# Moving 32 sums of weight quarters from VectorE to GpSimd at the turn between two groups, with a new order of copies and weighings on ScalarE

## The chip, the cores and the metric

The kernel runs on one core of one Trainium2 chip. The metric is the device time of one execution in microseconds (us), as the median over the runs; a profile of one execution stands beside it. The span of a profile is some 1.8 us shorter than the time.

## The reference

```python
def reference(x, w):                       # x: 8 x 2048 x 2048, w: 2048 x 2048, float32
    cs = np.cumsum(x, axis=1)
    diff = cs - shifted(cs)                # cut: the cumulative sum, less itself one row earlier
    return np.matmul(diff, w)
```

The difference of a cumulative sum is x again, so the kernel computes x times w: 16384 rows by 2048 by 2048.

## The kernel before

The kernel multiplies in 2x2 blocks with seven products in place of eight. A group is four row tiles of 128 rows, taken as two block rows. From the second group on, three of the seven products are themselves cut in 2x2, again with seven products; these need sums of the quarters of three weight blocks, B21, B22 and T4. Each set has 16 sums of 128 x 512 float16, made once, at the turn from the first group (`group_plain`) to the second (`second` in `group`).

Names: A11 to A22, B11 to B22 and C11 to C22 are blocks of x, w and the result. S1 to S4 are sums of blocks of x ("row sums"), T1 to T4 sums of blocks of w, Q1 to Q4 sums of the quarters of a weight block. X, Y, Z and V are pairs of PSUM banks, into which the products go (tile `b` in the profile; weights are `W`, quarter sums also `inner`). g and h mark the first row tile of each block row, u and v are row scales.

The engines: TensorE multiplies. ScalarE copies a product out of PSUM with a row scale ("keep"), weighs a row tile (sum of absolute values, which gives the row scales) and narrows it to float16. VectorE adds further products into the kept tile ("add") and makes all sums. The parts that matter, with cuts marked:

```python
    def keep(dst, ps, scale):                       # ScalarE, L497
        for c, p in pieces_of(dst, ps):
            after("act", lambda: nc.scalar.activation(c, p, COPY, scale=scale))
    def add(dst, ps, scale):                        # VectorE, L502: PSUM in, one SBUF tensor in
        ...
    def total(dst, p, q, op):                       # VectorE, L511: row sums S1, S2, ...
        after("dve", lambda: nc.vector.tensor_tensor(dst.all, p.all, q.all, op))
    def less(dst, p, q):                            # VectorE, L515: sums of weights, two SBUF tensors in
        for k in range(len(dst)):
            after("dve", lambda: nc.vector.tensor_tensor(dst[k], p[k], q[k], SUB))
    def less_in(Q1, Q2, Q4, t11, t12, t21, t22):    # 12 sums of a block's quarters
        less(Q1, t12, t11); less(Q2, t22, Q1); less(Q4, t21, Q2)
    def less_in3(Q1, Q2, Q4, t11, t12, t21, t22):   # 4 more, in place: Q3
        less(t12, t22, t12)
    def new_c(slot):                                # a tile of C in one of four slots
        return cpool.tile([P, NH], f32, name=f"c{slot}")
    ...
    # first group, near its end
    add(C22, X, vg)
    put(C22, g + 1, 1)                              # store of C22, slot d
    ...
    less(T4, B21, T2)
    product(Z, S1, T1, True)
    ...
    weigh(g + 5, c)                                 # waits for the load of row tile g + 5
    scale_of(g + 5)
    C22 = new_c(d)                                  # slot d again
    keep(C22, Z, vh)
    ...
    less_in(*in2); less_in3(*in2)                   # B21
    product(Z, S4h, B22, False)
    ...
    less_in(*in3)                                   # B22
    ...
    # second group
    product(X, A11g, B11, True)
    units[g], units[h] = unit(g), unit(h)           # scales u, on VectorE
    keep(C11g, X, ug)
    S3g = sums(g, S4g)                              # four row sums, S2 among them
    weigh(h + 1, c); ready(h + 1); less_in(*in4)    # T4
    ...
    product(X, S2, T2, False)
```

`after` keeps each engine's instructions in the order of the program, so an engine that waits for one instruction holds up all that stand behind it.

Of the kernel before, what the change touches and what calls it, by code (L numbers as in the profile page):

```python
# [33 lines left out]
def kernel(  # L34
# [6 lines left out]
    nc = tc.nc  # L41
# [12 lines left out]
    ADD = mybir.AluOpType.add  # L54
    SUB = mybir.AluOpType.subtract
    MUL = mybir.AluOpType.mult
    MAX = mybir.AluOpType.max
    AX = mybir.AxisListType
# [21 lines left out]
    B11, T1, B12, T2, B21, T3, B22, T4 = (  # L80
        [p[:, i // 2, i % 2] for p in pieces] for i in range(8)
    )
# [51 lines left out]
    def after(engine, ask):  # L134
        if engine in last:
            with tc.issue_after(last[engine].ins):
                said = ask()
        else:
            said = ask()
        last[engine] = said[-1] if isinstance(said, tuple) else said  # L140
        return said


    with tc.tile_pool(name="ring", bufs=7) as ring, tc.tile_pool(
# [97 lines left out]
        def put(c, rows, columns, queue=nc.gpsimd):  # L242
            return queue.dma_start(out2[rows, columns], c)
# [31 lines left out]
        for ko in range(KO - KQ):  # L275
# [9 lines left out]
            if ko in turns:  # L285
                q, a = turns[ko]
# [32 lines left out]
        x4, _ = after("sp", lambda: bring(PLAIN))  # L319
        x6, _ = after("sp", lambda: bring(PLAIN + 2))  # L320
# [25 lines left out]
        got = {}  # L346
# [68 lines left out]
        m = small.tile([P, 1], f32, name="m")  # L415
# [9 lines left out]
        x7, _ = after("sp", lambda: bring(PLAIN + 3))  # L425
# [39 lines left out]
    def product(ps, a, b, first):  # L465
        for k in range(KH):
            for n in range(NH // NB):
                nc.tensor.matmul(  # L468
                    ps[n],
                    a[k],  # L470
                    b[k][:, n, :],
                    start=(first and k == 0),
                    stop=(k == KH - 1),
                    skip_group_check=True,
                )
# [19 lines left out]
    def keep(dst, ps, scale):  # L495
        for c, p in pieces_of(dst, ps):
            after("act", lambda: nc.scalar.activation(c, p, COPY, scale=scale))  # L497
# [12 lines left out]
    def total(dst, p, q, op):  # L510
        after("dve", lambda: nc.vector.tensor_tensor(dst.all, p.all, q.all, op))  # L511

    def less(dst, p, q):
        for k in range(len(dst)):
            after("dve", lambda: nc.vector.tensor_tensor(dst[k], p[k], q[k], SUB))  # L515


    def less_in(Q1, Q2, Q4, t11, t12, t21, t22):
        less(Q1, t12, t11)
        less(Q2, t22, Q1)  # L520
        less(Q4, t21, Q2)

    def less_in3(Q1, Q2, Q4, t11, t12, t21, t22):
        less(t12, t22, t12)

    def new_c(slot):
        return cpool.tile([P, NH], f32, name=f"c{slot}")
# [5 lines left out]
    def fetch_x(t):  # L533
        if t < END:
            came[t], _ = after("sp", lambda: bring(t))

    def weigh(t, slot):
        if t < END:
            xf = came.pop(t)
            m, _ = after("act", lambda: measure(xf, new_c(slot)))  # L540
            got[t] = m, None, xf


    def weigh_in(t, ps):
        if t < END:
            xf = came.pop(t)
            m = small.tile([P, 1], f32, name="m")
            m4 = small.tile([P, 4], f32, name="m4")
            for i in range(4):
                at = ds(i * NB, NB)  # L550
                after(
                    "act",
                    lambda: nc.scalar.activation(  # L553
                        ps[i % 2],
                        xf[:, at],
                        ABS,
                        scale=1.0 / ROW,
                        accum_out=m4[:, i : i + 1],
                    ),
                )  # L560
            after("dve", lambda: nc.vector.tensor_reduce(m, m4, AX.X, ADD))  # L561
            got[t] = m, None, xf

    def scale_of(t):
        if t < END:
            m, _, xf = got[t]
            s, _ = after("dve", lambda: invert(m))
            came[t] = xf, s

# [25 lines left out]
    def sums_in(a, b, first, second):  # L595
        a11, a12, a21, a22 = a.half(0), a.half(1), b.half(0), b.half(1)
        s1, s2, s3, s4 = (p.half(n) for p in (first, second) for n in range(2))

        def half_one():
            total(s1, a21, a22, ADD)  # L600
            total(s2, s1, a11, SUB)

        def half_two():
            total(s3, a11, a21, SUB)
            total(s4, a12, s2, SUB)

        return half_one, half_two, (a11, a12, a22, s1, s2, s3, s4)
# [39 lines left out]
    def group_plain(g, X, Y, Z, V, a, b, c, d):  # L647
        h = g + 2
        ug, uh = unit(g), unit(h)
        A11g, A12g = parts(g)  # L650
        A11h, A12h = parts(h)
        A21g, A22g = parts(g + 1)
        product(X, A11g, B11, True)
        for k in range(3):
            block(B22, 1, 1, k, "act")
        C11g = new_c(a)
        keep(C11g, X, ug)
        for k in range(3, KH):
            block(B22, 1, 1, k, "act" if k < 6 else "dve")
        product(V, A12g, B21, True)  # L660
        product(Y, A11h, B11, True)
        add(C11g, V, ug)
        put(C11g, g, 0)

        less(T3[:2], B22[:2], B12[:2])
        total(S1, A21g, A22g, ADD)
        product(Z, A12h, B21, True)
        weigh(h + 1, d)
        C11h = new_c(b)
        keep(C11h, Y, uh)  # L670
        total(S2, S1, A11g, SUB)
        less(T2[:4], B22[:4], T1[:4])
        scale_of(h + 1)
        vg = unit(g + 1)
        ready(h + 1)
        turn(h + 1)
        fetch_x(h + 4)
        less(T2[4:], B22[4:], T1[4:])
        product(V, S1, T1, True)
        C22 = new_c(d)  # L680
        keep(C22, V, vg)
        less(T3[2:3], B22[2:3], B12[2:3])
        total(S4g, A12g, S2, SUB)
        product(X, S2, T2, False)
        C12g = new_c(c)
        keep(C12g, X, ug)
        total(A21g, A11g, A21g, SUB)
        less(T3[3:], B22[3:], B12[3:])
        product(V, S4g, B22, False)
        A21h, A22h = parts(h + 1)  # L690
        vh = unit(h + 1)
        weigh(g + 4, a)
        product(X, A21g, T3, False)
        total(S1, A21h, A22h, ADD)
        total(S2, S1, A11h, SUB)
        add(C11h, Z, uh)
        put(C11h, h, 0)
        scale_of(g + 4)
        ready(g + 4)
        turn(g + 4)  # L700
        add(C12g, V, ug)
        put(C12g, g, 1)
        fetch_x(g + 5)
        product(Y, S2, T2, False)
        C12h = new_c(a)
        keep(C12h, Y, uh)
        add(C22, X, vg)
        put(C22, g + 1, 1)
        total(S4h, A12h, S2, SUB)
        less(T4, B21, T2)  # L710
        product(Z, S1, T1, True)
        total(A21h, A11h, A21h, SUB)
        weigh(h + 4, b)
        scale_of(h + 4)
        ready(h + 4)
        turn(h + 4)
        fetch_x(h + 5)
        weigh(g + 5, c)
        scale_of(g + 5)
        C22 = new_c(d)  # L720
        keep(C22, Z, vh)
        product(X, A22g, T4, False)
        C21 = new_c(b)
        keep(C21, X, vg)
        ready(g + 5)
        turn(g + 5)
        put(C21, g + 1, 0)
        product(Y, A21h, T3, False)
        add(C22, Y, vh)
        put(C22, h + 1, 1)  # L730
        less_in(*in2)
        less_in3(*in2)
        product(Z, S4h, B22, False)
        add(C12h, Z, uh)
        put(C12h, h, 1)
        fetch_x(g + 8)
        less_in(*in3)
        product(Y, A22h, T4, False)
        C21 = new_c(c)
        keep(C21, Y, vh)  # L740
        put(C21, h + 1, 0)

    def group(g, X, Y, Z, V, a, b, c, d):
        h = g + 2
        second = g == PLAIN + 4
# [7 lines left out]
            units[g], units[h] = unit(g), unit(h)  # L753
        u = ug, uh = units.pop(g), units.pop(h)

        C11g = new_c(a)
        keep(C11g, X, ug)
        S3g = sums(g, S4g)
        if second:
            weigh(h + 1, c)  # L760
            ready(h + 1)
            less_in(*in4)
        turn(h + 1)
        fetch_x(h + 4)
        product(Y, A11h, B11, True)
        if second:
            weigh_in(g + 4, V)
        C11h = new_c(b)
        keep(C11h, Y, uh)
        if not second:  # L770
            weigh_in(g + 4, V)
        scale_of(g + 4)
        vg, vh = unit(g + 1), unit(h + 1)
        A21h, A22h = parts(h + 1)
        product(X, S2, T2, False)
        C12g = new_c(c)
        keep(C12g, X, ug)
        one, two, A2 = sums_in(A12g, A12h, S4h, S0)
        one()
        two()  # L780
# [5 lines left out]
        total(A21h, A11h, A21h, SUB)  # L786
        total(S2, S1, A11h, SUB)
        S3h = A21h
        product(X, S3g, T3, False)
        add(C22, X, vg)  # L790
        put(C22, g + 1, 1)
# [11 lines left out]
                ready(h + 4)  # L803

        inner_product(A2, in2, banks, C11g, C11h, *u, between_2)
        if second:
            less_in3(*in3)
            less_in3(*in4)
        total(S4h, A12h, S2, SUB)
        turn(h + 4)  # L810
        put(C11h, h, 0)
# [130 lines left out]
```

## Time and profile before

| | before |
|---|---|
| median of the runs | 1509.08 us (1508.40 to 1509.49, 4 runs) |
| span of the profile | 1507.3 us |
| TensorE busy | 1490.6 us (99%) |
| VectorE, ScalarE, GpSimd busy | 1104.4, 864.5, 5.2 us |
| TensorE's waits between 80 and 175 us | 2.8 us |

TensorE is full; what that leaves to be won is worked out in the prediction. Columns of a timeline: start, length, engine, line, operation, out and in with shape, count. One view the prediction did not show is VectorE's timeline at B21's sums and at the row sum S2 (columns: start, length, engine, line, operation, out and in with shape, count):

```profile
119.70 1.42 DVE L515 TENSOR_TENSOR W<-W 128x512 f16<-128x512 f16 x4
...
123.72 1.42 DVE L515 TENSOR_TENSOR W<-W,W 128x512 f16<-128x512 f16 x4
...
131.37 0.69 DVE L511 TENSOR_TENSOR W<-W,xT 128x1024 f16<-128x1024 f16 x1
```

Each sum lasts 0.42 us, and since they overlap a little, four take 1.42 us. All 16 run from 119.70 to 125.1 us: 5.4 us. S2 is ready at 132.06, half a microsecond before TensorE's first matmul with it (132.56).

### The profile page before, as it was taken

To read this page: it belongs to the slowest core of one execution; us is meant where nothing else is said; L and a number is where in the kernel's file an instruction comes from. 1 tells how busy PE (TensorE), PEld (TensorE's weight loads), DVE (VectorE), ACT (ScalarE), POOL (GpSimd) and SP (SyncE) were. 2 spreads that over 40 slices of the span, in tenths; PEclk is the share of its full clock that TensorE was granted. 3 is DMA by queue.
4 is the path that set the end of the run, shared out by engine and by line. 5 is a ranking of instruction groups with operands and counts; after the bars stand their busy time and mean duration, and the time that the engine had idled before them with its cause. 6 is when DMAs were issued, how large, how long until landed. Compare 5 with 4: busy or idle time off the path is not lost.

```text
span 1507.3 us, 19123 instructions
## 1 busy us (share of the span) xinstructions
PE 1490.6 (99%) x6911; PEld 673.8 (45%) x6911; DVE 1104.4 (73%) x2053; ACT 864.5 (57%) x1107; POOL 5.2 (0%) x12
## 2 busy tenths in 40 slices
PE   8999999999999999999999999999999999999998
PEld 3444444444444444444444444444444444444443
DVE  7997777776677676777676776766776767776767
ACT  5875655565655566555656555655555565556551
POOL 0100000000000000000000000000000000000000
PEclk9999999999999999999999999999999999999999
DMA  9988878878978987888789788878788888887772
GB/s 362 351 250 233 236 224 246 234 213 227 235 225 244 224 224 236 215 246 236 210 229 232 230 241 217 235 222 248 216 244 207 236 221 250 232 236 216 223 208 112
DMA packets 322479, 351.50 MB, mean 233 GB/s; under 512 B 266896, under 2 KB 266896, under 8 KB 306512
## 3 DMA queue, kind: packets, MB, share of 16 engines
q1 hardware_dynamic: 321536, 347.92, 81.1%
q0 software_dynamic: 560, 1.84, 0.3%
q8 instruction: 54, 0.88, 0.2%
q10 hardware_dynamic: 288, 0.52, 0.1%
q14 instruction: 41, 0.34, 0.1%
HBM read 150.99 MB, written 134.22 MB: 189 GB/s over the span
## 4 chain that ended last, share of the span: by engine, by line
PE 88%; DVE 1%; DMA 1%; issue 0%; ACT 0%; DVEq 0%; ACTq 0%; SPq 0%
PE b L468 52%; PE b L479 36%; DVE c L502 1%; DMA fin<-in_x_dram 0%; DMA xT<-fin 0%; DVE W L511 0%; ACT b L553 0%; DVE W L515 0%; ACT c L497 0%; DVEq L937 0%; DVE xT L511 0%; DVE s L112 0%; DVE m L111 0%; DVE u L586 0%; DVE m L561 0%
## 5 line engine op out<-in xcount | busy, mean ns | idle before, releaser
L502 DVE SCALAR_TENSOR_TENSOR c<-b,u,c 128x512 f32<-128x512 f32 (+1 forms) x883 | 675.0, 799 | 234.8 <-ACT c L497 112.8
L497 ACT ACTIVATE c<-b,u 128x512 f32<-128x512 f32 x496 | 314.5, 680 | 265.4 <-PE b L468 170.5
L468 PE MATMUL b<-W,xT 128*128 128x512 f16 x2048 | 462.1, 379 | 0.8 <-ACT c L497 0.8
L468 PE MATMUL b<-W,W 128*128 128x512 f16 x1764 | 411.7, 379 | 1.8 <-ACT c L497 1.5
L105 ACT ACTIVATE c<-fin 128x2048 f16<-128x2048 f32 x92 | 175.7, 1910 | 242.4 <-DMA out_dram<-c 220.5
L468 PEld LDWEIGHTS <-xT 128*128 128x128 f16 x2048 | 200.4, 98 | 242.6 <-issue 1.1
L468 PEld LDWEIGHTS <-W 128*128 128x128 f16 x2016 | 197.2, 98 | 240.2 <-issue 2.1
L116 ACT ACTIVATE fin<-fin,s 128x2048 f16<-128x2048 f32 x123 | 246.3, 2002 | 93.8 <-issue 50.8
L479 PEld LDWEIGHTS <-W 128*128 128x128 f16 x1560 | 152.1, 98 | 187.5 <-issue 2.5
L479 PE MATMUL b<-W,W 128*128 128x512 f16 x810 | 220.0, 379 | 1.0 <-DVE c L502 1.0
L479 PE MATMUL b<-W,xT 128*128 128x512 f16 x720 | 180.0, 379 | 0.0
L479 PE MATMUL b<-inner,W 128*128 128x512 f16 x660 | 176.2, 379 | 0.0
L479 PEld LDWEIGHTS <-xT 128*128 128x128 f16 x960 | 93.9, 98 | 113.3
L561 DVE TENSOR_REDUCE m<-m 128x1 f32<-128x4 f32 x29 | 4.6, 157 | 106.7 <-ACT b L553 106.7
L553 ACT ACTIVATE b<-fin 128x512 f32<-128x512 f32 x116 | 67.8, 585 | 14.5 <-DMA fin<-in_x_dram 14.5
L468 PE MATMUL b<-W 128*128 128x512 f16 x252 | 75.0, 379 | 0.0
L511 DVE TENSOR_TENSOR W<-W,xT 128x1024 f16<-128x1024 f16 x122 | 68.2, 559 | 3.2
L511 DVE TENSOR_TENSOR W<-xT,W 128x1024 f16<-128x1024 f16 x122 | 67.5, 553 | 0.0
L479 PE MATMUL b<-inner,xT 128*128 128x512 f16 x240 | 61.6, 379 | 0.0
L233 PE MATMUL b<-wb,xP 128*128 128x512 bf16 x240 | 55.4, 383 | 5.9 <-ACT wb L216 4.8
L511 DVE TENSOR_TENSOR W<-xT,xT 128x1024 f16<-128x1024 f16 (+1 forms) x92 | 54.8, 596 | 0.0
L111 DVE TENSOR_SCALAR m<-m 128x1 f32<-128x1 f32 x124 | 18.5, 149 | 34.6 <-ACT c L105 33.5
(54 smaller groups left out, 457.9 us busy)
## 6 DMA issues: line engine op xcount, KB each, us to landing
out_dram<-c SPq DMA_DIRECT2D x247, 512.0 KB, 3.1
fin<-in_x_dram SPq DMA_DIRECT2D x123, 1024.0 KB, 5.5
W<-in_w_dram SPq DMA_DIRECT2D x32, 512.0 KB, 9.6
W<-in_x_dram SPq DMA_DIRECT2D x16, 256.0 KB, 7.4
xT<-fin SPq DMA_TRANSPOSE x184, 5.2
out_dram<-o POOLq DMA_DIRECT2D x7, 256.0 KB, 3.9
out_dram<-o SPq DMA_DIRECT2D x7, 256.0 KB, 4.1
xP<-in_x_dram SPq DMA_DIRECT2D x1, 1024.0 KB, 5.1
```

The source lines that it names most:

```text
L105: return m, nc.scalar.activation(waste.bitcast(f16), xf, ABS, scale=1.0 / ROW, accum_out=m)
L111: nc.vector.tensor_scalar(m, m, TINY, None, MAX)
L116: return xh, nc.scalar.activation(xh, xf, COPY, scale=s)
L233: lambda: nc.tensor.matmul(ps[r][n], xP[:, r, ko, :], wb[h, ko][:, ds(n * NB, NB)], start=(ko == 0), stop=(ko == KO - 1),),
L468: nc.tensor.matmul(ps[n], a[k], b[k][:, n, :], start=(first and k == 0), stop=(k == KH - 1), skip_group_check=True,)
L479: nc.tensor.matmul(ps, a[k], b[k], start=(first and k == 0), stop=(k == 3), skip_group_check=True)
L497: after("act", lambda: nc.scalar.activation(c, p, COPY, scale=scale))
L502: "dve", lambda: nc.vector.scalar_tensor_tensor(c, p, scale, c, MUL, ADD)
L511: after("dve", lambda: nc.vector.tensor_tensor(dst.all, p.all, q.all, op))
L553: lambda: nc.scalar.activation(ps[i % 2], xf[:, at], ABS, scale=1.0 / ROW, accum_out=m4[:, i : i + 1],),
L561: after("dve", lambda: nc.vector.tensor_reduce(m, m4, AX.X, ADD))
```

## The change

It means to relieve VectorE at the turn: GpSimd, idle otherwise, makes the sums of B22 and T4. ScalarE copies C22 before a weighing that waits for a load, and weighs the next row tile at once in free PSUM banks; the weighing after that one moves behind the copies of C11h and C12 (cut from the diff, like the signatures of `less_in` and `less_in3`). The diff, cut to its core:

```diff
-    def less(dst, p, q):
+    def less(dst, p, q, engine="dve"):
+        by = {"dve": nc.vector, "pool": nc.gpsimd}[engine]
         for k in range(len(dst)):
-            after("dve", lambda: nc.vector.tensor_tensor(dst[k], p[k], q[k], SUB))
+            after(engine, lambda: by.tensor_tensor(dst[k], p[k], q[k], SUB))
 ...
+        C22 = new_c(d)
+        keep(C22, Z, vh)
         weigh(g + 5, c)
         scale_of(g + 5)
-        C22 = new_c(d)
-        keep(C22, Z, vh)
 ...
+        less_in(*in4, engine="pool")
         less_in(*in2)
         less_in3(*in2)
 ...
-        less_in(*in3)
         product(Y, A22h, T4, False)
+        less_in3(*in4, engine="pool")
+        less_in(*in3, engine="pool")
+        less_in3(*in3, engine="pool")
 ...
+        if second:
+            weigh_in(h + 1, V)
         C11g = new_c(a)
         keep(C11g, X, ug)
         S3g = sums(g, S4g)
         if second:
-            weigh(h + 1, c)
+            scale_of(h + 1)
             ready(h + 1)
-            less_in(*in4)
 ...
-        if second:
-            less_in3(*in3)
-            less_in3(*in4)
```

More of the change, by code (lines that the diff above doesn't have):

```diff
@@ L511, in total, with less_in, less_in3 @@
         after("dve", lambda: nc.vector.tensor_tensor(dst.all, p.all, q.all, op))
-    def less(dst, p, q):
+    def less(dst, p, q, engine="dve"):
+        by = {"dve": nc.vector, "pool": nc.gpsimd}[engine]
         for k in range(len(dst)):
-            after("dve", lambda: nc.vector.tensor_tensor(dst[k], p[k], q[k], SUB))
-    def less_in(Q1, Q2, Q4, t11, t12, t21, t22):
-        less(Q1, t12, t11)
-        less(Q2, t22, Q1)
-        less(Q4, t21, Q2)
-    def less_in3(Q1, Q2, Q4, t11, t12, t21, t22):
-        less(t12, t22, t12)
+            after(engine, lambda: by.tensor_tensor(dst[k], p[k], q[k], SUB))
+    def less_in(Q1, Q2, Q4, t11, t12, t21, t22, engine="dve"):
+        less(Q1, t12, t11, engine)
+        less(Q2, t22, Q1, engine)
+        less(Q4, t21, Q2, engine)
+    def less_in3(Q1, Q2, Q4, t11, t12, t21, t22, engine="dve"):
+        less(t12, t22, t12, engine)
     def new_c(slot):
@@ L560, in weigh_in @@
                 )
-            after("dve", lambda: nc.vector.tensor_reduce(m, m4, AX.X, ADD))
-            got[t] = m, None, xf
+            got[t] = m, m4, xf
     def scale_of(t):
         if t < END:
-            m, _, xf = got[t]
+            m, of_parts, xf = got[t]
+            if of_parts is not None:
+                after("dve", lambda: nc.vector.tensor_reduce(m, of_parts, AX.X, ADD))
             s, _ = after("dve", lambda: invert(m))
@@ L759, in group @@
         if second:
-            weigh(h + 1, c)
+            scale_of(h + 1)
             ready(h + 1)
-            less_in(*in4)
+            product(Y, A11h, B11, True)
+            C11h = new_c(b)
+            keep(C11h, Y, uh)
         turn(h + 1)
         fetch_x(h + 4)
-        product(Y, A11h, B11, True)
-        if second:
+        if not second:
+            product(Y, A11h, B11, True)
+            C11h = new_c(b)
+            keep(C11h, Y, uh)
             weigh_in(g + 4, V)
-        C11h = new_c(b)
-        keep(C11h, Y, uh)
-        if not second:
-            weigh_in(g + 4, V)
-        scale_of(g + 4)
+            scale_of(g + 4)
         vg, vh = unit(g + 1), unit(h + 1)
@@ L777, in group @@
         keep(C12g, X, ug)
+        if second:
+            weigh_in(g + 4, V)
         one, two, A2 = sums_in(A12g, A12h, S4h, S0)
@@ L788, in group @@
         S3h = A21h
+        if second:
+            scale_of(g + 4)
         product(X, S3g, T3, False)
@@ L805, in group @@
         inner_product(A2, in2, banks, C11g, C11h, *u, between_2)
-        if second:
-            less_in3(*in3)
-            less_in3(*in4)
         total(S4h, A12h, S2, SUB)
```

## The prediction

> **What bounds the kernel now.** I read the page first, for which engine is full.
>
> ```profile
> span 1507.3 us, 19123 instructions
> PE 1490.6 (99%) x6911; PEld 673.8 (45%) x6911; DVE 1104.4 (73%) x2053; ACT 864.5 (57%) x1107; POOL 5.2 (0%) x12
> PE 88%; DVE 1%; DMA 1%; issue 0%; ACT 0%; DVEq 0%; ACTq 0%; SPq 0%
> ```
>
> TensorE is busy for all but 16.7 us of the span, and the chain that ended last is nearly all its matmuls. A group of four row tiles repeats every 45.8 us and holds 212 matmuls, 0.216 us each; 6911 of them make about 1493 us. Nothing in this change removes a matmul, so it can only win idle time of TensorE. The second view, busy time in stretches of 20 us, says where that idle time lies: some 8 us in the first 60 us (loading and converting the weights), 2.8 us between 80 and 160 us, none in most of the 1300 us after, and some 5 us at the end. The change touches the turn from the first group (no inner recursion) to the second, so only the second place is open to it. The third view, the waits of TensorE from 80 to 175 us, puts a sum on it, and the timeline of TensorE shows each hole:
>
> ```profile
> PE b L468 <- ACT c L497: 2.3, 3, 1.3
> PE b L468 <- DVE W L511: 0.3, 1, 0.3
> PE b L479 <- DVE c L502: 0.2, 1, 0.2
> ...
> 118.39 0.38 PE L468 MATMUL b<-W,W 128*128 128x512 f16 x1 [1.32 <-ACT c L497]
> 118.97 1.24 PE L468 MATMUL b<-W,W 128*128 128x512 f16 x5 [0.20 <-ACT c L497]
> ...
> 140.63 3.61 PE L468 MATMUL b<-W,xT 128*128 128x512 f16 x16 [0.78 <-ACT c L497]
> ...
> 159.03 1.02 PE L479 MATMUL b<-W,W 128*128 128x512 f16 x4 [0.20 <-DVE c L502]
> ```
>
> The reader is to see four holes, 1.32 + 0.20 + 0.78 + 0.20 = 2.50 us, and who ends each. (The 0.3 us behind L511 comes at 96 us, before anything that the change moves.) The fourth view, ScalarE's timeline, gives the reason of the first three:
>
> ```profile
> 115.76 1.91 ACT L105 ACTIVATE c<-fin 128x2048 f16<-128x2048 f32 x1 [1.94 <-DMA fin<-in_x_dram]
> 117.67 2.40 ACT L497 ACTIVATE c<-b,u 128x512 f32<-128x512 f32 x4
> ...
> 130.78 1.26 ACT L497 ACTIVATE c<-b,u 128x512 f32<-128x512 f32 x2 [3.88 <-DVE u L586]
> 131.93 1.91 ACT L105 ACTIVATE c<-fin 128x2048 f16<-128x2048 f32 x1
> ...
> 138.76 3.54 ACT L497 ACTIVATE c<-b,u 128x512 f32<-128x512 f32 x6
> ```
>
> At 115.76 ScalarE weighs a row tile that had to wait for its load. The copy of C22 out of PSUM stands behind it and starts at 117.67, though its product had ended at 110. Later ScalarE stands idle for 3.88 us, because the scale u stands on VectorE behind the sums of B22's quarters; then two weighings and a narrowing delay the copies of C11 and C12 to 138.76, and TensorE waits for C12's bank.
>
> **What the Trainium skill says.** "GPSIMD Engine Reference", section 3.1, gives 4497 ns for a two-input operation of 2048 elements on GpSimd. My estimate from it is a quarter, about 1.1 to 1.2 us, for 512. No trace here has that operation; VectorE's own takes 0.34 us per instruction (x8 in 2.77 us). "SBUF — State Buffer", section "Who interferes with whom", says that a VectorE instruction with two SBUF inputs contends with a GpSimd instruction that reads SBUF, and that whichever starts first blocks the other for a whole instruction. VectorE's sums all have two SBUF inputs; its accumulations of a PSUM bank into C have one. The trace of before can't show it: GpSimd is idle after 65 us. "GPSIMD Engine Reference", section 2.1, adds about 6 us at the first call of a newly loaded GpSimd routine; the built kernel has a load between the last GpSimd transfer (64 us) and the first sum (from 107 us), so this should be hidden.
>
> **The change, part by part.**
>
> 1. C22 kept ahead of the weighing. ScalarE ends its narrowing at 113.8 us, and both halves of C22 can be out at 113.8 + 1.25 = 115.1 us, before TensorE wants the bank at 117.07. This removes 1.32 + 0.20 = 1.52 us. The weighing stays where the load puts it (115.76), so nothing behind it is later.
>
> 2. Sums to GpSimd: 32 instructions (16 for T4, 16 for B22) of 128x512. VectorE loses 12 (126.4 to 130.4), 12 (134.2 to 138.2) and 8 (153.4 to 156.0), in all about 10.8 us. It is not the bound, so this counts only through the scale u, the first sums S1, S2 and the add at 159.03.
>
> 3. Weighing in free PSUM banks at once. With u out early, the order on ScalarE becomes: weigh the tile as soon as it is loaded (4 x 0.61, about 2.5 us, from 125.4), copy C11 (127.9 to 129.1), narrow, copy C11h, copy C12. With the 1.5 us of part 1, TensorE ends the product for C11 at 127.5 and needs its bank at 131.0; it ends the product for C12 at 134.5, whose copy ends at 135.7. The next product on that bank comes at 137.9. The 0.78 us go. The two orders of instructions also show that the first inner product's matmul is put behind that product, so the next weighing in the same PSUM banks (to about 138.1) is out of its way until 141.
>
> 4. The add at 159.03 stands on VectorE behind eight sums of 2.7 us that leave, so its 0.20 us go.
>
> Sum: at best 2.50 us, 1508.95 - 2.5 = 1506.45. Moving the small reduction of the four part sums to the place of the scale changes nothing in later groups: on every engine the instruction orders agree there.
>
> **The rivals.**
>
> A. GpSimd is late. It can start when T4's first piece is there (106.6), but VectorE makes T4 in one run until 110.8; I count from 111. Sixteen sums for T4 at 1.2 us end at 130, those of B22 at 149.4. The inner product with B22's sums begins at about 154.4 after the gain; it needs the last of Q4 at 158.7 and Q3 at 159.6. Thus 10 us of slack, or up to 1.5 us per instruction. If GpSimd also stands back for VectorE's two-input sums in that time (16 for B21, 4 + 4 + 3 for rows, about 12 us), it ends at 161.4 and TensorE waits about 2 us: 1508.5. At 2 us per instruction it would end at 175: some 15 us lost, 1521. T4's inner product comes at about 174, far behind its sums.
>
> B. VectorE is held up by GpSimd. S2 is needed at 131.0; VectorE without blocking has it at 119.6 + 16 x 0.34 + 1.3 (add to C12h) + 0.3 + 1.4 = 128. The slack is 3 us. Between 119 and 131 stand 18 two-input sums. If only the first of each run meets a GpSimd instruction, that is two times at most 1.2 us: hidden. If the two alternate one by one, each of the 18 waits about 1.1 us, some 20 us; less the 3 of slack, TensorE loses about 17 us: 1523. For it speaks the skill's rule; against it, that VectorE's sums run with no gap between them (8 in 2.77 us), so that GpSimd would hardly get in between.
>
> C. The gain is eaten later by a load. The DMA engines are 80 to 90% busy, but TensorE's own waits show none on a row tile after 180 us; I expect the 2.5 us to last to the end.
>
> **Range and chances.** I give about 45% to the full gain (1506.5), 25% to a small wait on GpSimd or a small blocking (1507 to 1509), 25% to B or a slow GpSimd (1511 to 1523), the rest to something unseen. The middle is 1507.0, the range 1505.7 to 1515, since nothing lower is there to be won and the upper side has the long tail. Faster by 2% would need 30 us, where TensorE idles 16.7 us in all: 0.003. Slower by 2% would need more than the worst rival gives: 0.012. Within 2%: 0.985.
>
> **What would show it.** Right: no wait of TensorE on a copy at about 117 and 138; C22's copy at about 114 on ScalarE; idle of ScalarE before C11 below 1 us; the next group starting 2.5 us earlier than 176.5; GpSimd's sums 1.1 to 1.3 us apart and ended by 155. Wrong: a wait of TensorE on GpSimd in the inner product at 155 to 161 (A), VectorE's 128x512 sums at well over 0.42 us each and TensorE waiting on L511 at 131 (B), a new wait on a transfer later (C). The estimate most likely to fail is the time of a GpSimd sum, the one duration that no trace here has, and the blocking with it.

## The result, and the profile after

The changed kernel takes 1525.51 us (1525.15 to 1526.27, 4 runs) against 1509.08: 16.4 us more. The ratio is 1.011, 95% interval 1.0092 to 1.0128. Counted at 2%, that is "same"; counted in microseconds, it is well outside the predicted range, which ended at 1515.

The page of the kernel after, and TensorE's waits from 80 to 185 us (columns of the waits: in total, times, longest):

```profile
span 1523.6 us, 19144 instructions
PE 1493.9 (98%) x6905; PEld 674.8 (44%) x6911; DVE 1112.7 (73%) x2022; ACT 865.2 (57%) x1113; POOL 49.9 (3%) x44
...
PE b L468 <- DVE W L511: 14.7, 2, 14.3
PE b L479 <- DVE c L502: 2.1, 1, 2.1
PE b L468 <- ACT c L497: 0.8, 2, 0.6
```

TensorE now waits 14.3 us at one place for a row sum of VectorE (L511), which was no wait at all before. Its timeline shows the holes in order:

```profile
118.33 0.38 PE L468 MATMUL b<-W,W 128*128 128x512 f16 x1 [0.63 <-ACT c L497]
...
147.07 1.03 PE L468 MATMUL b<-W,W 128*128 128x512 f16 x2 [14.26 <-DVE W L511]
...
163.82 0.59 PE L479 MATMUL b<-W,W 128*128 128x512 f16 x2 [2.12 <-DVE c L502]
```

The hole at 140 us is gone, the one at 118 us is smaller but still there, and two new ones have come. Why the row sum was late is told by VectorE's timeline:

```profile
122.37 4.91 DVE L516 TENSOR_TENSOR W<-W 128x512 f16<-128x512 f16 x4
...
137.55 5.24 DVE L516 TENSOR_TENSOR W<-W,W 128x512 f16<-128x512 f16 x4
142.71 1.40 DVE L502 SCALAR_TENSOR_TENSOR c<-b,u,c 128x512 f32<-128x512 f32 x2
...
145.49 1.52 DVE L511 TENSOR_TENSOR W<-W,xT 128x1024 f16<-128x1024 f16 x1
```

The same sums of B21 that took 1.42 us by fours take 5.24 us by fours. All 16 run from 122.37 to 142.8 us: 20.4 us in place of 5.4. The instructions themselves last longer, with no idle time before them, so this is no wait for a semaphore; and they read B21's quarters, which GpSimd doesn't touch. The two adds at 142.71, which read PSUM and one SBUF tensor, take 1.40 us as before, although GpSimd is at work. S2 (the line at 145.49) ends at 147.0, and TensorE goes on at 147.07. GpSimd's timeline beside it:

```profile
107.50 8.93 POOL L516 TENSOR_TENSOR inner<-W 128x512 f16<-128x512 f16 x4 [43.51 <-PE b L468]
116.40 9.30 POOL L516 TENSOR_TENSOR inner<-W,inner 128x512 f16<-128x512 f16 x8
125.67 5.22 POOL L516 TENSOR_TENSOR W<-W,W 128x512 f16<-128x512 f16 x4
```

GpSimd works without a gap from 107.5 to 152.4 us. Alone, its sums last 1.15 us each and come 1.11 us apart; with VectorE's among them (5.22 us by fours) they come 1.30 us apart, and so do VectorE's. In that stretch each VectorE sum gets in once per GpSimd sum. ScalarE shows the other half:

```profile
117.59 1.26 ACT L497 ACTIVATE c<-b,u 128x512 f32<-128x512 f32 x2 [3.16 <-DMA out_dram<-c]
118.74 1.91 ACT L105 ACTIVATE c<-fin 128x2048 f16<-128x2048 f32 x1
...
144.31 1.26 ACT L497 ACTIVATE c<-b,u 128x512 f32<-128x512 f32 x2 [14.88 <-DVE u L588]
```

C22's copy is ahead of the weighing now, but waits for a store until 117.59, hardly earlier than the 117.67 of before; and the weighing behind it starts at 118.74 in place of 115.76. The copy of C11 waits 14.88 us for the scale u behind VectorE's sums.

**The balance.** The third group starts at 193.25 us and not at 176.48: 16.77 us later. Of these, 0.63 us were there before the turn (X's product with T4 starts at 110.63, not 110.00). In the turn, the holes sum to 0.63 + 0.20 + 14.26 + 2.12 = 17.21 us against 2.50, which is 14.71 more. The rest is slower matmuls: the 32 after the long hole take 147.07 to 155.28 = 8.21 us and not 6.91, which is 1.30, and 48 others 0.15. The sum is 0.63 + 14.71 + 1.30 + 0.15 = 16.79. The granted clock from 146 to 152 us was 0.69. After the third group's start nothing is lost: 1330.4 us to the end, 1330.8 before.

### The profile page after: what moved, and what is told of

Its sections match the earlier page's. It is cut to its first block, busy times and chain, and to the rows that moved or that the text cites. A ratio compares the mean times of both kernels' runs of the same rounds, so it can differ in the third digit from the quotient of the medians.

```text
span 1523.6 us, 19144 instructions
## 1 busy us (share of the span) xinstructions
PE 1493.9 (98%) x6905; PEld 674.8 (44%) x6911; DVE 1112.7 (73%) x2022; ACT 865.2 (57%) x1113; POOL 49.9 (3%) x44
## 3 DMA queue, kind: packets, MB, share of 16 engines
q0 software_dynamic: 560, 1.84, 0.3%
## 4 chain that ended last, share of the span: by engine, by line
PE 89%; DVE 2%; ACT 0%; issue 0%; DVEq 0%; ACTq 0%
PE b L468 53%; PE b L479 36%; DVE W L516 1%; DVE c L502 0%; DVE inner L516 0%; DVE W L511 0%; ACT c L497 0%; DVE xT L511 0%; ACT b L554 0%; ACT c L105 0%; DVEq L945 0%; DVE m L111 0%; DVE s L112 0%; DVE u L588 0%; DVE m L568 0%
## 5 line engine op out<-in xcount | busy, mean ns | idle before, releaser
L511 DVE TENSOR_TENSOR W<-W,xT 128x1024 f16<-128x1024 f16 x122 | 69.8, 572 | 3.2
L511 DVE TENSOR_TENSOR W<-xT,W 128x1024 f16<-128x1024 f16 x122 | 68.3, 559 | 0.0
L511 DVE TENSOR_TENSOR W<-xT,xT 128x1024 f16<-128x1024 f16 (+1 forms) x92 | 55.2, 600 | 0.0
```

## The experiments

**Which part costs it?** My theory (T): VectorE's sums with two SBUF inputs wait for GpSimd's, and that is the loss. Rival (R): the new order on ScalarE costs most of it. Two runs take one part each.

The order alone:

```diff
-        less_in(*in4, engine="pool")
 ...
+        less_in(*in3)
         product(Y, A22h, T4, False)
-        less_in3(*in4, engine="pool")
-        less_in(*in3, engine="pool")
-        less_in3(*in3, engine="pool")
 ...                                   # in the second group, as before:
+            less_in(*in4)
 ...
+            less_in3(*in3)
+            less_in3(*in4)
```

> ScalarE's new order alone: all sums back on VectorE, where the kernel before has them. Theory T (VectorE's two-input sums wait for one GpSimd instruction each, and that alone costs the 16 us): about the time of before, 1508 to 1510, TensorE's waits at the turn of the groups 2 to 4 us, VectorE's 128x512 sums 0.33 us apart. Rival R (the new order on ScalarE, with C22 waiting for the slot's store, costs most of it): 1515 or more.

Measured: 1511.81 us against 1509.58 in the same rounds, 2.2 us slower (ratio 1.0016, interval 1.0001 to 1.0031). R is out as the main cause, but my 1508 to 1510 was too good. TensorE's timeline:

```profile
134.00 0.69 PE L468 MATMUL b<-W,W 128*128 128x512 f16 x2 [1.97 <-DVE W L511]
...
135.34 3.97 PE L468 MATMUL b<-W,W 128*128 128x512 f16 x12
```

The weighing that C22's copy holds up makes VectorE start B21's sums 1.9 us later (121.59, not 119.70), and TensorE waits 1.97 us for S2. Twelve matmuls then take 3.97 us, where 2.75 is usual: the granted clock was 0.72 from 135 to 140 us. The wait was thus followed by some 1.7 us of slower matmuls (the 32 from 134.00 to 142.60 take 8.60 us, not 6.91); that the wait caused them is likely, but no run tests it.

The sums on GpSimd alone, in the kernel before (its `less` with an engine, as in the change):

```diff
+        less_in(*in4, engine="pool")
         less_in(*in2)
         less_in3(*in2)
 ...
-        less_in(*in3)
         product(Y, A22h, T4, False)
+        less_in3(*in4, engine="pool")
+        less_in(*in3, engine="pool")
+        less_in3(*in3, engine="pool")
 ...                                   # and the 20 sums of the second group taken out
```

> The kernel before with nothing but the 32 sums on GpSimd. Theory T: 1523 to 1529, VectorE's B21 sums 1.3 us apart, TensorE waiting 12 to 16 us for the row sums (line of total). Rival R: within 4 us of before.

Measured: 1523.74 us against 1509.58, 14.2 us slower (ratio 1.0095, interval 1.0078 to 1.0111). TensorE's waits:

```profile
PE b L468 <- DVE W L511: 12.4, 2, 11.6
```

B21's 16 sums run from 120.62 to 140.9 us, 1.27 us each, and TensorE waits 11.6 us for the row sum. As T expected, but for this wait, just under its 12 us. The two parts, 2.2 and 14.2 us, add up to the 16.4 of the whole, in part by luck: TensorE's added waits in the turn are 0.58, 11.51 and 14.71 us in the three runs, and its slower matmuls 1.84, 1.95 and 1.45 us.

**Is it GpSimd's reading?** Each sum on GpSimd is replaced by three fills of the same output, which read nothing. Its output is wrong, which doesn't matter for the time.

```diff
-            after(engine, lambda: by.tensor_tensor(dst[k], p[k], q[k], SUB))
+            for _ in range(3) if engine == "pool" else ():
+                after(engine, lambda: by.memset(dst[k], 0.0))
+            if engine == "dve":
+                after(engine, lambda: by.tensor_tensor(dst[k], p[k], q[k], SUB))
```

> The changed kernel with each of the 32 GpSimd sums replaced by three fills of the same output, which write SBUF and read nothing (the result is wrong on purpose). If what blocks VectorE is GpSimd's reading (theory T): VectorE's B21 sums run at 0.33 us while GpSimd is busy, no wait of TensorE on them, time 1506 to 1510. If it is GpSimd's being busy with SBUF at all: sums well over 0.5 us each and 1514 or more.

Measured: 1507.99 us (1507.02 to 1509.14) against 1509.16, within noise of before (ratio 0.9993, interval 0.9979 to 1.0006). GpSimd's and VectorE's timelines:

```profile
123.20 6.59 POOL L517 MEMSET W<- 128x512 f16 x12 [16.35 <-PE b L468]
129.73 19.66 POOL L517 MEMSET inner<- 128x512 f16 x36
...
126.59 1.42 DVE L519 TENSOR_TENSOR W<-W,W 128x512 f16<-128x512 f16 x4
```

GpSimd fills without a gap from 123.2 to 155.9 us, and VectorE's sums in that time take 1.42 us by fours, as with GpSimd idle. What blocks VectorE's two-input sums is GpSimd's reading of SBUF, not its being at work. That a fill is shorter than a sum (0.53 us, not 1.15) is not the reason: in the next run GpSimd's instructions of 0.68 us block VectorE more than the long ones. A GpSimd instruction with one SBUF input was not tried.

**How long does one wait for the other?** GpSimd's sums in halves of 256 columns:

```diff
+            for at in (ds(0, NB // 2), ds(NB // 2, NB // 2)) if engine == "pool" else ():
+                after(engine, lambda: by.tensor_tensor(dst[k][:, at], p[k][:, at], q[k][:, at], SUB))
```

> The changed kernel with each GpSimd sum cut into two of 256 columns: the same work, 64 instructions. If VectorE waits for a whole GpSimd instruction (theory T): its B21 sums come about 0.7 to 0.8 us apart and not 1.3, the row sum S2 is ready some 9 us sooner, time 1513 to 1518. If the two engines share the bandwidth in proportion (rival S): spacing stays at 1.2 to 1.3 us and the time at 1524 to 1527.

Measured: 1537.04 us against 1509.58. Both expectations failed. VectorE's and GpSimd's timelines:

```profile
122.14 30.08 DVE L519 TENSOR_TENSOR W<-W 128x512 f16<-128x512 f16 x1
...
126.85 5.06 POOL L517 TENSOR_TENSOR W<-W,W 128x256 f16<-128x256 f16 x8
```

VectorE's first sum of B21 lasts 30.08 us, until GpSimd has ended (151.9 us). GpSimd's halves come 0.63 us apart, the same as with VectorE not waiting: VectorE did not get in once. So "one VectorE sum per GpSimd instruction" is not a rule. With GpSimd's instructions at 512 columns it gets in between them, at 256 columns it did not.

Then VectorE's 16 sums of B21 in halves, GpSimd's whole:

```diff
-        less_in(*in2)
-        less_in3(*in2)
+        less_in(*in2, engine="halves")      # VectorE, each sum as two of 256 columns
+        less_in3(*in2, engine="halves")
```

> The changed kernel with VectorE's 16 sums of B21 cut into 32 of 256 columns; GpSimd's stay at 512. If VectorE gets in once per GpSimd sum, however short its own is: the halves come 1.3 us apart too, GpSimd ends at about 152 us with some 23 of them done, S2 some 10 us later, time 1533 to 1538. If the two share time by the amount of work: halves 0.65 us apart and 1524 to 1528.

Measured: 1530.77 us against 1509.16 (ratio 1.0143, interval 1.0127 to 1.0158). VectorE's and GpSimd's timelines:

```profile
122.16 9.22 DVE L517 TENSOR_TENSOR W<-W 128x256 f16<-128x256 f16 x8
...
134.67 9.30 POOL L521 TENSOR_TENSOR inner<-W,inner 128x512 f16<-128x512 f16 x8
```

The halves come 1.15 us apart, as GpSimd's sums do, where they come 0.20 us apart once GpSimd has ended: at both sizes tried, VectorE waits for a whole GpSimd sum. The time is 2 us under the expected range because the halves hold GpSimd up less (its sums come 1.16 us apart, not 1.30), so that GpSimd ended at 148.6 us and not at 152.

**Does it help to be first?** In the changed kernel GpSimd's first sum started at 107.50 but lasted 5.59 us, while VectorE made T4 and one row sum (106.59 to 112.1). VectorE's and GpSimd's timelines:

```profile
106.59 4.89 DVE L516 TENSOR_TENSOR W<-W 128x1024 f16<-128x1024 f16 x8
...
107.50 5.59 POOL L516 TENSOR_TENSOR inner<-W 128x512 f16<-128x512 f16 x1 [43.51 <-PE b L468]
```

I thought that a run of VectorE keeps GpSimd out, and held GpSimd until B21's first sum was made:

```diff
+        gate = small.tile([P, 1], f16, name="gate")
+        after("pool", lambda: nc.gpsimd.tensor_tensor(gate, in2[0][0][:, :1], in2[0][0][:, :1], SUB))
+        less_in(*in3, engine="pool"); less_in3(*in3, engine="pool")    # B22 first
+        less_in(*in4, engine="pool"); less_in3(*in4, engine="pool")
```

> The same 32 sums on GpSimd, but the first held until VectorE has made its first B21 sum (a GpSimd instruction of one column that reads it), and B22's sums ahead of T4's. If the engine that is already in a run without gaps keeps the other out, as VectorE's T4 run did (first GpSimd sum 5.6 us): B21's 16 sums run at 0.33 us, GpSimd gets in at about 128 us at the add, the four row sums are slowed by at most 3 us, time 1507 to 1511. If the engines alternate whoever comes first: B21's sums again 1.3 us apart and 1522 to 1527.

Measured: 1525.62 us against 1509.58, no better than the change. VectorE's and GpSimd's timelines:

```profile
122.07 1.42 DVE L516 TENSOR_TENSOR W<-W 128x512 f16<-128x512 f16 x4
123.40 2.67 DVE L516 TENSOR_TENSOR W<-W,W 128x512 f16<-128x512 f16 x2
...
122.58 0.30 POOL L741 TENSOR_TENSOR gate<-W 128x1 f16<-128x1 f16 x1 [58.29 <-DVE W L516]
123.27 5.12 POOL L516 TENSOR_TENSOR inner<-W 128x512 f16<-128x512 f16 x4 [0.39 <-PE b L468]
```

VectorE's first four sums took 0.42 us each. GpSimd's first real sum started at 123.27, and from the fifth on, at 123.40, VectorE's came 1.3 us apart again. So being first did not protect a run of 512-column sums, while the run of 1024-column sums of T4 did hold GpSimd off. (That the first GpSimd sum of the changed kernel lasted 5.59 us because it was the first call of its kind is out: here the gate is that first call, and it took 0.30 us.) The width alone does not decide either: the changed kernel's row sums, of 1024 columns too, came in turn with GpSimd's and lasted 1.18 to 1.64 us instead of 0.69. What decides who gets in next is open: the runs show three outcomes (VectorE alone, in turn, GpSimd alone) and not the rule behind them.

**Can a version beat both?** In the next three runs GpSimd makes no sums, the order on ScalarE stays new, and I took the holes one by one. Each diff is against the run before; the first, against the run with the order alone, puts 12 of B22's sums behind the scale and the row sums of the second group:

```diff
-        less_in(*in3)                       # first group
 ...
             ready(h + 1)                    # second group, after sums(g, S4g)
+            less_in(*in3)
             less_in(*in4)
```

> No sums on GpSimd; the new ScalarE order; and on VectorE the first three sums of B22 behind the scale and the row sums of the second group, not ahead. The wait on S2 (2.0 us in the run with the new order alone) should go, C22's hole of 0.7 to 0.8 us stays: 1507.5 to 1509.5 where before is at 1509.3, 1 to 2 us less than before at best.

Measured: 1509.83 us against 1509.16 (ratio 1.0005, interval 0.9992 to 1.0017): no difference clear of noise, where 1507.5 to 1509.5 was expected. The wait on S2 is down to 0.2 us, but the 24 sums now stand ahead of the adds, and TensorE waits 1.88 us for these at 147 us. A wait took the place of the one removed.

Then the store of the earlier C22, which C22's slot waits for, ahead of a load in the queue:

```diff
-        fetch_x(g + 5)
         product(Y, S2, T2, False)
         C12h = new_c(a)
         keep(C12h, Y, uh)
         add(C22, X, vg)
         put(C22, g + 1, 1)
+        fetch_x(g + 5)
```

> As the run with the row sums first, and the store of the earlier C22 goes into the queue ahead of the next row tile's load. If C22's copy waited for that store alone (slot of C), it starts at 113 to 115 us and not at 117.5, the hole at 118 us goes, the weighing is back at about 116: 1506.5 to 1508, 1.5 to 2.5 us less than before. If the slot isn't what it waited for, no difference from the run without it.

Measured: 1508.17 us against 1509.16 (ratio 0.9992, interval 0.9980 to 1.0005), not clear of noise and just above the expected 1506.5 to 1508. But ScalarE's timeline settles the question of the slot:

```profile
113.93 1.25 ACT L497 ACTIVATE c<-b,u 128x512 f32<-128x512 f32 x2
116.54 1.91 ACT L105 ACTIVATE c<-fin 128x2048 f16<-128x2048 f32 x1 [1.36 <-DMA fin<-in_x_dram]
```

C22 is copied at 113.93, where the prediction had it, and the holes at 118 us are gone. What is left in the turn is 1.39 us for the late adds.

Third, eight of T4's sums, Q4 and Q3, moved behind the inner product with B22's sums, still on VectorE:

```diff
-            less_in(*in4)
+            less(Q1, t12, t11); less(Q2, t22, Q1)      # of in4
 ...
-            less_in3(*in4)
 ...                                         # after the inner product A3
+            less(in4[2], in4[5], in4[1])               # Q4
 ...                                         # before the store of C21g
+                less_in3(*in4)
```

> As the run with the store first, no sums on GpSimd, but eight of T4's sixteen sums moved on VectorE behind the inner product with B22's sums, where they are still in time (Q4 wanted at about 169 us, Q3 at 174). The hole of 1.39 us at 145.6, behind the late adds, should go: 1506.5 to 1507.5 where before is at 1509.2. If VectorE is short there anyway, a new wait on the adds at 168 to 175 takes its place and the time stays at 1508.

Measured: 1506.83 us against 1509.43 (ratio 0.9980, interval 0.9966 to 0.9994). TensorE waits 0.28 us in the whole turn. This is clear of noise: 2.6 us faster than before, the size of the gain that the change was after.

Last, the other eight, Q1 and Q2 of T4, on GpSimd, but only once the second row's S2 is made, when VectorE has nothing but adds for a while:

```diff
-            less(Q1, t12, t11); less(Q2, t22, Q1)      # behind ready(h + 1)
 ...
             scale_of(g + 4)
+            gate, edge = small.tile([P, 1], f16, name="gate"), S2.all[:, 0, :1]
+            after("pool", lambda: nc.gpsimd.tensor_tensor(gate, edge, edge, SUB))
+            less(Q1, t12, t11, "pool"); less(Q2, t22, Q1, "pool")
```

> As the run with the sums spread, but the other eight of T4's sums (Q1, Q2) on GpSimd, held until VectorE has made the second row's S2 at about 143 us, since from there to 152 us VectorE has only adds with one SBUF input. If only VectorE's two-input sums contend (theory T): the adds stay at 0.66 to 0.70 us each, GpSimd's sums come 1.16 us apart, no new wait of TensorE, and the time equals that of the spread sums to within 1 us. If GpSimd at work slows VectorE's adds too: adds above 0.9 us, a wait of TensorE on L502 of several us, 1511 or more.

Measured: 1506.18 us (1505.83 to 1506.29) against 1509.43 (ratio 0.9976, interval 0.9964 to 0.9989). GpSimd's and VectorE's timelines:

```profile
142.72 4.51 POOL L516 TENSOR_TENSOR inner<-W 128x512 f16<-128x512 f16 x4 [0.50 <-PE b L479]
147.18 4.51 POOL L516 TENSOR_TENSOR inner<-W,inner 128x512 f16<-128x512 f16 x4
...
142.33 2.92 DVE L502 SCALAR_TENSOR_TENSOR c<-b,u,c 128x512 f32<-128x512 f32 x4
...
150.69 2.30 DVE L516 TENSOR_TENSOR W<-W,W 128x512 f16<-128x512 f16 x4
```

The four adds take 2.92 us, as they do without GpSimd, and GpSimd's sums come 1.1 us apart: neither slows the other. Only at 150.69, where GpSimd's last sum meets VectorE's next two-input ones, four of these take 2.30 us in place of 1.42, and nobody waits for them. This version is 3.2 us faster than before and some 19 us faster than the change. Whether it beats the sums spread on VectorE by its 0.65 us is not sure: the two intervals overlap.

## Why the prediction was wrong

The step that failed is in rival B: "against it, that VectorE's sums run with no gap between them (8 in 2.77 us), so that GpSimd would hardly get in between". I let this weigh against the rule on contention that I had quoted myself, and gave B and a slow GpSimd together 25%; the range ended at 1515, below the 1523 of rival B's own sum. The runs showed that GpSimd, once in, keeps its turn: VectorE's sums came one per GpSimd sum (1.3 us), and the run held back on purpose showed that a run of 512-column sums without gaps gives no protection. So the 10.8 us that VectorE was to be relieved of came back as 15.0 us on B21's sums alone, ahead of the row sum that TensorE waits for.

As far as the fills stand for sums without blocking, the gain would have been 1.2 us and not 2.5 (1507.99 against 1509.16, within noise): 0.83 us stay at C22 and 0.27 us at late adds.

Point by point:

- **What bounds the kernel** was right: TensorE, with 2.5 us to be won. After the turn, nothing was lost or won (rival C did not come).
- **Part 1, C22 early**, failed. I looked at when the product ended and when ScalarE was free, and not at C22's slot, whose last tile was still being stored. The copy came at 117.59 and not at 113.8, so 0.83 us of the hole stayed. "Nothing behind it is later" was wrong as well: the weighing came 3 us later, and the run with the order alone, where it does so too, was 2.2 us slower than before. With the store put first, the step came out as predicted (113.93).
- **Part 2, the time of a GpSimd sum**: 1.1 to 1.2 us estimated from the Trainium skill ("GPSIMD Engine Reference", section 3.1), 1.15 us measured alone. No extra time at the first call was seen: the gates, the first of their kind on GpSimd, took 0.30 and 0.20 us. The estimate that I called the most likely to fail held; the blocking named beside it did not.
- **Part 3**: the hole at 140 us is gone, but not by the step I gave. The scale u came later, not earlier, since it stands behind B21's slowed sums. The fills that read nothing show the step as I meant it: there C11 is copied at 129.9 us (127.9 was predicted) and the hole at 140 us is gone too. (The copies at 138.76 that the prediction calls C11's and C12's are C11h's and C12's; C11 is copied at 130.78.)
- **Part 4**: the 0.20 us at 159 went. The new 2.12 us are for other adds, those of the inner product before that one (without a wait at 146.67 in the kernel before), as VectorE was still late.
- **Rival A** did not come: GpSimd ended at 152.4, and the inner product with B22's sums began at 174 without a wait. Even on the undisturbed schedule (155 to 160) it would have been in time.
- **Rival B** was the right mechanism and close in size: 17 us estimated, 14.26 us of wait measured. The two-input sums of B21 came 0.94 us longer each (15.0 us over 16, where 1.1 us each was assumed) and the two row sums up to S2 1.3 us longer together. The slack was 2 us and not 3: with the fills S2 is ready at 130.89 and its first matmul starts at 132.84. This makes 15.0 + 1.3 - 2 = 14.3 us. Its time of 1523 lacked the slower matmuls after the idle time (1.3 us) and the new hole of 2.12 us.

## What to carry to other kernels

A free engine is not free room: before moving work to GpSimd, see what VectorE does in the same stretch, and if that has two SBUF inputs, and GpSimd's instructions read SBUF, count on each of its instructions waiting for one of GpSimd's, or for all of them, as here. Eight of the same sums cost TensorE nothing when they were held until VectorE had only instructions with one SBUF input. When an instruction is moved up in an engine's order, ask what else it waits for, its output's slot included, since everything behind it will wait too.

## What the Trainium skill lacked or had wrong

- "SBUF — State Buffer", section "Who interferes with whom", has the mechanism right: two-input VectorE sums waited on GpSimd's sums (0.42 to 1.37 us each) and not on fills that only write (0.42), and adds with one SBUF input were not slowed (0.75 us each). It lacks who gets in next. With 512-column GpSimd sums VectorE got in after each; with 256-column ones it waited 30.08 us, for all of them; T4's run of 1024-column VectorE sums stretched GpSimd's first sum to 5.59 us, but row sums as wide came in turn with GpSimd's.
- "GPSIMD Engine Reference", section 3.1, has a measured time of the two-input operation for 2048 float32 elements only, beside a rate per element. For 128x512 float16 these runs show 1.15 us alone (1.11 us from one to the next), near a quarter of its time, and for 256 columns 0.68 us (0.63), more than half of that. So each instruction has a fixed part of about 0.15 us (an estimate: twice 0.63 less 1.11), for which the section has no figure.
- "TensorE: Matmul & The Clock Gate", section "Why this matters for your kernels", asks for no idle gaps of over about 3 us. In the one trace of the run with the new order alone, a wait of 1.97 us was followed by a granted clock of 0.72 over 135 to 140 us; waits of 1.88 and 1.39 us in two other runs were not followed by a dip. So slower matmuls came once after a gap shorter than the page's; whether the gap was the cause, and what decides, no run shows.
